# Attention scores as 128-row matmuls of zero-padded queries, with masks and biases added by VectorE

## The chip, the cores and the metric

The kernel runs on one core of one Trainium2 chip. The metric is device time in microseconds (us), the median of the runs of one build. Engines are called by the names of the profile: PE (TensorE matmul), PEld (the weight loads of TensorE, which overlap PE), DVE (VectorE), ACT (ScalarE), POOL (GpSimd), SP (SyncE, which issues most DMAs).

## The reference, cut to what matters

Two transformer blocks over 256 tokens of width 1024, float32. Block 1 has two layers. A layer projects its input into five branches (sparse, latent and differential attention, a gated unit, attention over a memory), gates, merges and adds them. Block 2 has a gated linear attention, a block-sparse attention with relative-position biases, a modulation from a condition vector, and an MLP. The attentions have 8 heads over 256 keys. Four of them add something to the scores ahead of the softmax:

```
differential, latent:  s = (q . k) * scale ; s = where(key <= query, s, -inf) ; p = softmax(s)
sparse:                s = (q . k) * scale ; s = where(key among the 64 chosen, s, -inf) ; p = softmax(s)
block-sparse (moba):   s = (q . k) * scale + bias[head, query, key] ; p = softmax(s)
```

Query and key have 64 dimensions in the sparse, differential and block-sparse attention, and 96 in the latent one. The sparse attention chooses its keys by an index score, made of 4 heads of 64 dimensions.

## The kernel before, in words

**The weight stream.** Every projection is cut into pieces of 512 rows by up to 512 columns of weights. A piece is loaded by SP (L359, L362), split by ACT into a rounded high part `wh` (L377) and by DVE into the rest `wl` (L378), and multiplied by PE in three products: high by high (L427), low weight by high operand (L428), high weight by low operand (L430), or L440, L442 and L443 in the other orientation. Six pieces are loaded ahead and three split ahead. Operands (the transposed rows of x) are split in the same way (ACT L575, DVE L576).

**What runs beside it.** Three lanes hold generators with everything else: preparation of queries and keys, attention, merging. After each half of a piece the program takes a step in a lane, so a few instructions of attention stand between two half pieces in the order of every engine. Engines work through their order in sequence; a scheduler can move instructions by their due times when the program is built.

**Attention.** `attention()` (L620) takes units. A unit is a tile t of 128 queries and two heads (t = 1, 256 keys) or four (t = 0, only the first 128 keys count), so that its scores fill one bank of PSUM, 512 floats a row. `soft()` calls `score` for each head, takes the row maximum over the bank (L640) and its negative times the scale (L642), and lets ACT write the exponentials with their sums (L647). One step later the exponentials are transposed on PE (L668) and copied out (ACT L671, DVE L672); one step further they multiply the values (L688). A differential unit calls `soft` twice. The memory's attention goes through the same code, with a scale that is a tile and no mask.

**Scores.** Queries and keys lie transposed, two heads of 64 dimensions on the 128 partitions. A head of 64 dimensions takes its half of the partitions: `qT[hb, ...]` against `kT[hb, ...]`, a matmul over 64 rows of the array (L938 differential, L926 sparse t = 0, L1391 moba, L894 the index). The heads of one unit lie on the same half, since they are two apart. For t = 1 the sparse attention's queries and keys are stacked as high and low parts on all 128 rows (L609, L610). The mask is added on PE by a bf16 matmul of an identity with a mask tile into the same bank: `identb` by `cmb` (L939, differential and latent), `identb` by `mb[t]` (L927, sparse). Moba's bias is added by DVE into a new tile (L637).

**The start.** POOL builds constants and then issues the DMAs of the small vectors (`first_loads`: positions, frequencies and eight vectors of gains and biases, L184 to L189), the last of which are transposed into `gT` (L211). Operand 1 of the first piece is transposed from the first half of x, operand 2 from the second half, whose DMA comes later.

Of the kernel before, what the change touches and what calls it, by code (L numbers as in the profile page):

```python
# [9 lines left out]
F32 = mybir.dt.float32  # L10
# [27 lines left out]
class Lane:  # L38
    """Work that runs beside the weight stream, a step at a time."""
# [18 lines left out]
def block_kernel(ctx: ExitStack, tc: tile.TileContext, a, out):  # L58
# [30 lines left out]
    def work(shape, tag="wk", dt=F32, bufs=None):  # L89
        n = 1  # L90
        for s in shape[1:]:
            n *= s
        own = tag in ("gains0", "gains1", "mb0", "mb1")
# [29 lines left out]
    class Operand:  # L123
        """[128 rows of K, up to 4 tiles, 256 tokens] as the sum of two float32r parts."""
# [9 lines left out]
    def urgent(f):  # L134
        """f with what it issues before what else is ready."""
# [21 lines left out]
    # ---- constants  # L157
    ident = cst.tile([128, 128], F32, name="ident")
    identb = cst.tile([128, 128], BF, name="identb")
    cmb = cst.tile([128, 128], BF, name="cmb")  # L160
# [38 lines left out]
    V.tensor_copy(identb, ident)  # L199
# [3 lines left out]
    V.tensor_scalar(cmb, cmf[:, 128:], -BIG * 0.5, MASK, op0=OP.is_lt, op1=OP.mult)  # L203
# [14 lines left out]
    def rsqrt(v, n):  # L218
        """1/sqrt of a [128, n] tile by Newton steps from a guess of the exponent's halving."""
# [17 lines left out]
    # ---- angles  # L237
# [42 lines left out]
    def rope(v, tab, half):  # L280
        """v [128, 2, heads, >= 2 half], in place on its first 2 half columns."""
# [14 lines left out]
    # ---- the weight stream  # L296
# [33 lines left out]
    def spread(first, fns):  # L330
        """Pieces that fns add, placed evenly among those from first on."""
# [91 lines left out]
    def mm_tok(ps, xo, k0, hi, lo, nk, n, first, last, t):  # L423
        """ps[128 tokens, n] += the tokens' rows of xo (K tiles k0..) times the weights."""
# [8 lines left out]
    def mm_tr(ps2, xo, hi, lo, nk, first, last, evac):  # L433
        """ps2: two banks of [128 columns, 2 column tiles, 256 tokens]."""
# [14 lines left out]
    def chunk(ap, ops, c0, n, evac, r0=0, pre=None, post=None):  # L449
        """Columns c0..c0+n of ap times the operands (4 K tiles each); evac(t, psum)."""  # L450
# [18 lines left out]
    def chunk_by_tile(ap, ops, c0, n, evac, pre=None, post=None, mid=None):  # L469
        """As chunk, with both K halves of the first 128 tokens before those of the others."""  # L470
# [27 lines left out]
    def chunk_pair(ap, ops, cols, evacs, pres=None, post=None, rows=(0, 512), by_tile=False):  # L498
        """Two chunks whose K halves alternate; by_tile: at the end the first 128 tokens come first."""
# [44 lines left out]
    # ---- transposes into operands  # L544
# [6 lines left out]
    def to_operand(src, t, xo, n=4, g=None, scale=None, k0=0):  # L551
        """src [128 tokens, n * 128] -> K tiles k0.. of xo, times a gain per row or a number."""
# [12 lines left out]
    def to_operand_g(srcs, xo, n, g, step=None):  # L565
        """srcs: two row tiles [128 tokens, n * 128] -> the K tiles of xo, times a gain per row."""
# [14 lines left out]
    def to_operand_mod(src, t, xo, am, bm, k0):  # L581
        """Transposes of src times am[:, k] plus bm[:, k]."""
# [24 lines left out]
    def stacked_mm(ps, q, hi, lo, stop=True):  # L607
        """ps = q^T (hi + lo), for q with a high and a low part and hi, lo repeated on both halves of the rows."""
        T.matmul(ps, q, hi, start=True, stop=False)  # L609
        T.matmul(ps, q, lo, start=False, stop=stop)  # L610
# [8 lines left out]
    # ---- softmax attention, one bank of scores at a time  # L619
    def attention(units, finish, nheads, dv, d=1):  # L620
        """units: (t, heads, nk, score, scale, combine, av, bias); one step works on three units."""
# [7 lines left out]
        def soft(u, heads):  # L629
            """Exponentials of one bank of scores, and the reciprocals of their sums."""  # L630
# [4 lines left out]
            if u.get("bias") is not None:  # L635
                sb = work([128, nh, nk])
                V.tensor_tensor(sb, ps, u["bias"], OP.add)  # L637
                ps = sb
            mx, rs, sm = small(nh), small(nh), small(nh)
            V.reduce_max(mx, ps, AX.X)  # L640
            if isinstance(u["scale"], float):
                V.tensor_scalar(mx, mx, -u["scale"], None, op0=OP.mult)  # L642
            else:
                V.tensor_scalar(mx, mx, u["scale"], -1.0, op0=OP.mult, op1=OP.mult)
            p = work([128, nh, nk])
            for k in range(nh):
                A.activation(p[:, k, :], ps[:, k, :], AF.Exp, bias=mx[:, k:k + 1], scale=u["scale"],  # L647
                             accum_out=sm[:, k:k + 1])
# [63 lines left out]
    # ---- state of a layer  # L712
# [5 lines left out]
    # block 1: the memory's keys and values  # L718
# [43 lines left out]
    # block 1: one layer  # L762
    def layer(l, h):
# [4 lines left out]
        def entry():  # L768
            """The scale of the layer's input rows."""
# [11 lines left out]
        # --- gated unit  # L781
# [46 lines left out]
        # --- memory  # L828
# [935 lines left out]
```

## Time and profile before

| | |
|---|---|
| median of 3 runs | 1260.48 us (1260.02 to 1261.89) |
| span of the profiled execution, first to last instruction | 1258.0 us |
| mean granted TensorE clock, share of full speed | 0.989 |
| PE busy | 1238.1 us, 98% |
| DVE busy | 908.2 us, 72% |
| ACT busy | 653.9 us, 52% |
| POOL busy | 11.4 us, 1% |
| moved by DMA | 231.31 MB, 184 GB/s in the mean |

The profiled execution's own time is what its span shows; the runs lie 2.0 to 3.9 us above the span, so a change of the span is taken for the same change of the time. Busy time of PE counts a matmul's whole latency, and neighbours overlap: two matmuls of one kind in a row take less than their two durations. What an instruction costs the stream is read from the distance between starts, not from its duration.

### The profile page before, as it was taken

Reading aid. Unit: us, or ns where it says so; the run is one execution under the profiler, and the core shown is the slowest. Engines: PE = TensorE matmul, PEld = TensorE weight load, DVE = VectorE, ACT = ScalarE, POOL = GpSimd, SP = SyncE. Lnnn points to the kernel's source line nnn. Section 1 sums busy time; section 2 is a strip of 40 time slices with the busy share of each in tenths; the row PEclk is TensorE's granted clock in tenths of the full one; section 3 lists DMA queues with packets and bytes.
Section 4 is the critical chain, followed back from the end, with each engine's and each line's share of the span. In section 5 each row is a group of like instructions: output and inputs, shape, how many; then the busy total and the mean of one; then the engine's idle time right before and its main releaser. Section 6 shows DMA issues by size and latency. Waiting matters only on the chain.

```text
span 1258.0 us, 17257 instructions
## 1 busy us (share of the span) xinstructions
PE 1238.1 (98%) x6593; PEld 1051.2 (84%) x6593; DVE 908.2 (72%) x1755; ACT 653.9 (52%) x1149; POOL 11.4 (1%) x29
## 2 busy tenths in 40 slices
PE   7999999999999999999999999999999999999997
PEld 6899888887888888898888878888878777899995
DVE  6876779757886777776886677876685867847665
ACT  5744644546565455545444655654555555545442
POOL 2000000000000000000000000000000000000000
PEclk8999999999999999999999999999998999999999
DMA  8965465454475465754566434755447725666750
GB/s 270 318 208 172 135 222 193 144 168 134 140 234 178 135 224 180 247 168 167 189 209 191 141 122 151 234 168 166 155 152 254 271 76 167 200 188 226 242 183 34
DMA packets 121283, 231.31 MB, mean 184 GB/s; under 512 B 5420, under 2 KB 17008, under 8 KB 121072
## 3 DMA queue, kind: packets, MB, share of 16 engines
q1 hardware_dynamic: 120880, 230.12, 55.6%
q8 instruction: 52, 0.85, 0.3%
q0 software_dynamic: 320, 0.08, 0.1%
q14 instruction: 31, 0.25, 0.1%
HBM read 229.10 MB, written 2.63 MB: 184 GB/s over the span
## 4 chain that ended last, share of the span: by engine, by line
PE 95%; DVE 2%; ACT 1%; DMA 1%; issue 0%; SPq 0%; ACTq 0%
PE pm L427 23%; PE pm L428 23%; PE pm L430 23%; PE pm L440 3%; PE pm L442 3%; PE pm L443 3%; PE po L688 3%; PE pm L548 3%; PE pm L938 2%; PE pm L668 2%; DMA t<-in_x_dram 1%; PE pm L939 1%; PE pm L836 1%; PE pm L1391 1%; PE pm L926 1%; PE po L430 1%
## 5 line engine op out<-in xcount | busy, mean ns | idle before, releaser
L378 DVE TENSOR_TENSOR wl<-wt,wh 128x1024 fp32r<-128x1024 f32 (+3 forms) x386 | 443.1, 1175 | 170.7 <-ACT wh L377 170.2
L427 PE MATMUL pm<-wh,hi 128*128 128x512 f32 (+4 forms) x1320 | 520.0, 395 | 4.5 <-ACT hi L594 2.5
L377 ACT ACTIVATE wh<-wt 128x1024 fp32r<-128x1024 f32 (+3 forms) x386 | 379.3, 1020 | 277.7 <-PE pm L430 172.2
L428 PE MATMUL pm<-wl,hi 128*128 128x512 f32 (+4 forms) x1320 | 509.6, 387 | 0.0
L430 PE MATMUL pm<-wh,lo 128*128 128x512 f32 (+4 forms) x1320 | 348.3, 384 | 0.0
L427 PEld LDWEIGHTS pm<-wh,hi 128*128 128x128 f32 x1320 | 251.3, 190 | 53.9 <-ACT hi L594 4.7
L428 PEld LDWEIGHTS pm<-wl,hi 128*128 128x128 f32 x1320 | 251.4, 191 | 44.4 <-DVE lo L576 0.2
L430 PEld LDWEIGHTS pm<-wh,lo 128*128 128x128 f32 x1320 | 246.5, 189 | 47.7
L440 PE MATMUL pm<-hi,wh 128*128 128x256 f32 x352 | 100.2, 285 | 0.0
L442 PE MATMUL pm<-lo,wh 128*128 128x256 f32 x352 | 99.4, 283 | 0.0
L443 PE MATMUL pm<-hi,wl 128*128 128x256 f32 x352 | 99.4, 283 | 0.0
L440 PEld LDWEIGHTS pm<-hi,wh 128*128 128x128 f32 x352 | 67.5, 192 | 0.5 <-ACT hi L575 0.2
L442 PEld LDWEIGHTS pm<-lo,wh 128*128 128x128 f32 x352 | 67.4, 192 | 0.5 <-DVE lo L576 0.2
L443 PEld LDWEIGHTS pm<-hi,wl 128*128 128x128 f32 x352 | 67.4, 192 | 0.0
L647 ACT ACTIVATE w<-pm,s 128x256 f32<-128x256 f32 (+1 forms) x96 | 39.2, 417 | 53.7 <-DVE s L642 52.1
L1320 DVE SCALAR_TENSOR_TENSOR w<-wt,cact,w 128x512 f32<-128x512 f32 x84 | 62.7, 746 | 1.9 <-DMA wt<-in_w_ada_dram 0.7
L688 PEld LDWEIGHTS po<-t,w 128*128 128x128 f32 x352 | 45.9, 191 | 3.5 <-ACT t L1563 0.7
L1134 ACT ACTIVATE t<-pm,s 128x512 f32<-128x512 f32 x40 | 27.6, 689 | 41.0 <-PE pm L430 40.3
L688 PE MATMUL po<-t,w 128*128 128x64 f32 (+1 forms) x352 | 45.1, 270 | 0.5 <-ACT t L1563 0.5
L548 PE MATMUL pm<-ident,t 128*128 128x128 f32 (+1 forms) x332 | 44.0, 273 | 1.6 <-DVE t L1270 1.6
L548 PEld LDWEIGHTS pm<-ident,t 128*128 128x128 f32 (+1 forms) x332 | 38.5, 137 | 7.7 <-issue 2.7
L617 ACT ACTIVATE j<-t 128x512 f32<-128x512 f32 (+3 forms) x60 | 28.9, 481 | 27.9 <-DVE t L1671 14.1
(285 smaller groups left out, 1052.5 us busy)
## 6 DMA issues: line engine op xcount, KB each, us to landing
wt<-in_w_in_dram SPq DMA_DIRECT2D x99, 1024.0 KB, 5.0
wt<-in_w_ff_dram SPq DMA_DIRECT2D x32, 1024.0 KB, 5.8
wt<-in_w_ada_dram SPq DMA_DIRECT2D x24, 1024.0 KB, 5.2
wt<-in_w_branch_dram SPq DMA_DIRECT2D x20, 1024.0 KB, 5.3
wt<-in_w_out_dram SPq DMA_DIRECT2D x12, 1024.0 KB, 5.1
wt<-in_mem_w_kv_dram SPq DMA_DIRECT2D x8, 1024.0 KB, 7.7
wt<-in_w_in_dram SPq DMA_DIRECT2D x4, 904.0 KB, 5.6
wt<-in_w_in_dram SPq DMA_DIRECT2D x4, 768.0 KB, 5.7
```

What stands on the lines that cost most here:

```text
L377: pin(A.activation(hv[:, ks], wv[:, ks], AF.Copy), on)
L378: pin(V.tensor_tensor(lv[:, ks], wv[:, ks], hv[:, ks].bitcast(F32), OP.subtract), on)
L427: T.matmul(ps[:, :n], xh, hi[:, i, :n], start=first and i == 0, stop=False)
L428: T.matmul(ps[:, :n], xh, lo[:, i, :n], start=False, stop=False)
L430: T.matmul(ps[:, :n], xo.lo[:, k0 + i, tsl(t)], hi[:, i, :n], start=False, stop=last and i == nk - 1)
L440: T.matmul(ps, wh, xh, start=first and i == 0 and c % 2 == 0, stop=False, skip_group_check=True)
L442: T.matmul(ps, wh, xl, start=False, stop=False, skip_group_check=True)
L443: T.matmul(ps, wl, xh, start=False, stop=last and i == nk - 1, skip_group_check=True)
L548: T.transpose(ps[:, i, :], src[:, i * w:(i + 1) * w], ident)
L647: A.activation(p[:, k, :], ps[:, k, :], AF.Exp, bias=mx[:, k:k + 1], scale=u["scale"], accum_out=sm[:, k:k + 1])
L688: T.matmul(opsum[t][:, h, :], pt[:, k * nb + b, :], u["v"](h, b), start=b == 0, stop=b == nb - 1)
L1320: V.scalar_tensor_tensor(acc, w[:, i, :], B["c"][:, k:k + 1], acc, op0=OP.mult, op1=OP.add)
```

## The change

Queries of 64 dimensions are written into tiles whose other 64 rows are zero (`qz` for the differential attention and moba, `dz` for the sparse attention's first tile and its index), and multiply the keys of both heads on all 128 rows. The zeros are written once by POOL; `padded()` writes only the rows that hold queries, one ACT instruction for each half. The mask matmuls and their two bf16 tiles are gone. The causal mask and the choice of keys (also used as tiles before, `cmf` and `mb`) and moba's bias are added by DVE's `tensor_tensor_reduce`, one instruction a head, which writes -scale times the sum to SBUF and its row minimum to `mx`; ACT's exponential then reads SBUF. The memory's attention keeps the old path. The scratch space of POOL's DMAs is set to 2048 bytes a partition (16384 by default).

```diff
+    qz = cst.tile([128, 8, 256], F32, name="qz")
+    dz = cst.tile([128, 12, 128], F32, name="dz")
+    for b, z in ((0, slice(64, 128)), (1, slice(0, 64))):
+        G.memset(qz[z, 4 * b:4 * b + 4, :], 0.0)
+        G.memset(dz[z, 4 * b:4 * b + 4, :], 0.0)
+        G.memset(dz[z, 8 + 2 * b:8 + 2 * b + 2, :], 0.0)
...
+    def padded(dst, ps, scale=1.0):
+        n = ps.shape[1]
+        for b in range(2):
+            own = slice(64 * b, 64 * b + 64)
+            A.activation(dst[own, n * b:n * b + n, :], ps[own], AF.Copy, scale=scale)
...
-            if u.get("bias") is not None:
-                sb = work([128, nh, nk])
-                V.tensor_tensor(sb, ps, u["bias"], OP.add)
-                ps = sb
             mx, rs, sm = small(nh), small(nh), small(nh)
-            V.reduce_max(mx, ps, AX.X)
-            if isinstance(u["scale"], float):
-                V.tensor_scalar(mx, mx, -u["scale"], None, op0=OP.mult)
+            p = work([128, nh, nk])
+            bias = u.get("bias")
+            if bias is not None:
+                for k in range(nh):
+                    V.tensor_tensor_reduce(out=p[:, k, :], in0=ps[:, k, :], in1=bias(k), scale=-u["scale"],
+                                           scalar=3.0e38, op0=OP.add, op1=OP.min, accum_out=mx[:, k:k + 1])
+                for k in range(nh):
+                    A.activation(p[:, k, :], p[:, k, :], AF.Exp, bias=mx[:, k:k + 1], scale=-1.0,
+                                 accum_out=sm[:, k:k + 1])
             else:
...
-                    A.activation(q0[:, 0:4, :], ps, AF.Copy)
+                    padded(dz[:, 0:8, :], ps)
...
-                    T.matmul(ps, q0[hb, hh // 2, :], q0[hb, 4, :], start=True, stop=False)
-                T.matmul(ps, identb, mb[t], start=False, stop=True)
+                    T.matmul(ps, dz[:, i, :], q0[:, 0, :], start=True, stop=True)
...
-        def causal(ps, q, k, t):
-            T.matmul(ps, q, k, start=True, stop=False)
-            T.matmul(ps[:, t * 128:(t + 1) * 128], identb, cmb, start=False, stop=True)
+        def causal(t):
+            return lambda k: cmf[:, 128 * (1 - t):]
...
-                ps = transpose4(cq[:, t, :])
-                A.activation(qT[:, :, tsl(t)], ps, AF.Copy)
+                padded(qz[:, :, tsl(t)], transpose4(cq[:, t, :]))
...
-                causal(ps, qT[hb, hh // 2, tsl(t)], kT[hb, hh // 2, 0:nk], t)
+                T.matmul(ps, qz[:, 4 * (hh % 2) + hh // 2, tsl(t)], kT[:, hh // 2, 0:nk], start=True, stop=True)
...
-    nc = bacc.Bacc("TRN2", target_bir_lowering=False, num_devices=1)
+    nc = bacc.Bacc("TRN2", target_bir_lowering=False, num_devices=1, dynamic_dma_scratch_size=2048)
```

Moba and the index are changed in the same way. In the changed kernel a line's number is 4 to 15 higher than before.

How the order changes, at three places. On PE, at the first differential unit of layer 1, the half piece ahead and then two heads of each of the unit's two banks; `t_2476` and `t_2477` are queries and keys. Before:

```order
L430 MATMUL pm_2631<-wh_2490,lo_130 128x288 x4
L938 MATMUL pm_2689<-t_2477,t_2476 128x256
L939 LDWEIGHTS identb
L939 MATMUL pm_2689<-cmb,identb 128x128
...
L938 MATMUL pm_2703<-t_2477,t_2476 128x256
```

And now:

```order
L434 MATMUL pm_2627<-wh_2487,lo_134 128x288 x4
L988 MATMUL pm_2685<-t_2473,qz 128x256 x2
L988 MATMUL pm_2697<-t_2473,qz 128x256 x2
L431 MATMUL pm_2628<-wh_2487,hi_133 128x288
```

The four heads' matmuls stand one behind the other, with no mask and no weight load of its own between them; the half pieces around them are the same.

On DVE, at the same unit, with the splits of weights (`wl`) around it. Before:

```order
L378 TENSOR_TENSOR wl_2768<-wt_2576,wh_2767 128x1024 x2
L640 TENSOR_REDUCE s_2694<-pm_2689 128x2
L642 TENSOR_SCALAR s_2694<-s_2694 128x2
L649 RECIPROCAL s_2695<-s_2696 128x2
L640 TENSOR_REDUCE s_2708<-pm_2703 128x2
L642 TENSOR_SCALAR s_2708<-s_2708 128x2
L378 TENSOR_TENSOR wl_2776<-wt_2629,wh_2775 128x1024
```

And now:

```order
L382 TENSOR_TENSOR wl_2760<-wt_2572,wh_2759 128x1024 x2
L653 ISA w_2691,s_2688<-pm_2685,cmf 128x256
L653 ISA s_2688 128x1
...
L664 RECIPROCAL s_2689<-s_2690 128x2
L653 ISA w_2703,s_2700<-pm_2697,cmf 128x256
L653 ISA s_2700 128x1
...
L382 TENSOR_TENSOR wl_2768<-wt_2625,wh_2767 128x1024
```

Each reduce with its small scaling became two pairs of instructions (four where a bank holds four heads); the second of a pair reads the accumulator into `mx`. The neighbours stayed.

On ACT, at the start, where `hi_127` and `hi_129` (before) are the operands of the first and second half of x and `wh_158` is the first piece. Before:

```order
L377 ACTIVATE wh_158<-wt_131 128x512 [waits DMAHW5_49]
L575 ACTIVATE hi_129<-pm_242,gT 128x256 [waits PE_49]
L575 ACTIVATE hi_127<-pm_173,gT 128x256 [waits DVE_49]
L377 ACTIVATE wh_158<-wt_131 128x512 [waits DMAHW6_49]
L377 ACTIVATE wh_186<-wt_138 128x1024 [waits DMAHW1_49]
```

And now, with `hi_131` and `hi_133` for the two operands and `wh_162` for the first piece:

```order
L381 ACTIVATE wh_162<-wt_135 128x512 [waits DMAHW5_49]
L579 ACTIVATE hi_131<-pm_177,gT 128x256 [waits DVE_49]
L381 ACTIVATE wh_162<-wt_135 128x512 [waits DMAHW6_49]
L381 ACTIVATE wh_190<-wt_142 128x1024 [waits DMAHW1_49]
...
L381 ACTIVATE wh_196<-wt_154 128x1024
L579 ACTIVATE hi_133<-pm_246,gT 128x256 [waits PE_49]
```

The second operand's first part, which waits for transposes of the second half of x, moved from ahead of the first piece's last part to behind the splits of the next two pieces. On PE those transposes moved in the same way behind 14 matmuls of the first piece, and on POOL the six fills stand ahead of the ten DMAs of `first_loads`.

## Rows read from the trace of the kernel before

**Rows 1.** The page, busy time of each engine.

```profile
PE 1238.1 (98%) x6593; PEld 1051.2 (84%) x6593; DVE 908.2 (72%) x1755; ACT 653.9 (52%) x1149; POOL 11.4 (1%) x29
```

**Rows 2.** Timeline of PE, a differential unit, 256 keys: start, duration, instructions.

```profile
285.15 0.70 PE L938 MATMUL pm<-t,t 64*128 64x256 f32 x2
285.78 0.23 PE L939 MATMUL pm<-cmb,identb 128*128 128x128 bf16 x1
285.94 0.70 PE L938 MATMUL pm<-t,t 64*128 64x256 f32 x2
...
288.40 0.30 PE L428 MATMUL pm<-wl,hi 128*128 128x288 f32 x1
```

**Rows 3.** Timeline of PEld at the same unit.

```profile
285.77 0.10 PEld L939 LDWEIGHTS <-identb 128*128 128x128 bf16 x1 [0.33 <-issue]
```

**Rows 4.** Timeline of PE, memory attention: 128 rows, 256 keys.

```profile
123.16 1.02 PE L836 MATMUL pm<-t,t 128*128 128x256 f32 x4
...
124.25 0.40 PE L428 MATMUL pm<-wl,hi 128*128 128x512 f32 x1
```

**Rows 5.** Timeline of PE, gated unit: 128 rows, 128 columns.

```profile
89.57 1.06 PE L817 MATMUL pm<-t,t 128*128 128x128 f32 x8
...
90.58 0.28 PE L442 MATMUL pm<-lo,wh 128*128 128x256 f32 x1
```

**Rows 6.** Timeline of PE, a sparse unit of four heads, 128 keys.

```profile
259.33 0.48 PE L926 MATMUL pm<-t 64*128 64x128 f32 x2
...
261.83 0.39 PE L428 MATMUL pm<-wl,hi 128*128 128x512 f32 x1
```

**Rows 7.** Timeline of PE, a latent unit of two heads, 256 keys.

```profile
383.47 0.59 PE L938 MATMUL pm<-t,t 96*128 96x256 f32 x2
...
384.79 0.40 PE L428 MATMUL pm<-wl,hi 128*128 128x512 f32 x1
```

**Rows 8.** Timeline of PE, a moba unit of two heads, 256 keys.

```profile
1002.49 1.13 PE L1391 MATMUL pm<-t,t 64*128 64x256 f32 x4
...
1003.88 0.40 PE L428 MATMUL pm<-wl,hi 128*128 128x512 f32 x1
```

**Rows 9.** Timeline of PE, index scores: two heads each of the two halves.

```profile
158.01 0.72 PE L894 MATMUL pm<-t 64*128 64x128 f32 x8
...
159.00 0.39 PE L428 MATMUL pm<-wl,hi 128*128 128x512 f32 x1
```

**Rows 10.** Groups of DVE and ACT by line and form: busy, mean ns, idle before.

```profile
L640 DVE TENSOR_REDUCE s<-pm 128x2 f32<-128x512 f32 x32 | 21.8, 682 | 3.6 <-PE pm L939 2.3 <-PE pm L927 1.3
L642 DVE TENSOR_SCALAR s<-s 128x2 f32<-128x2 f32 x28 | 4.7, 168 | 0.8
L637 DVE TENSOR_TENSOR w<-pm,t 128x512 f32<-128x512 f32 x6 | 4.1, 690 | 2.9 <-PE pm L1391 1.8 <-PE pm L1497 1.0
L576 DVE SCALAR_TENSOR_TENSOR lo<-pm,gT,hi 128x256 fp32r<-128x256 f32 x26 | 11.8, 477 | 5.7 <-ACT hi L575 5.7
L559 DVE SCALAR_TENSOR_TENSOR lo<-pm,gT,hi 128x128 fp32r<-128x128 f32 x16 | 4.5, 336 | 0.1
L647 ACT ACTIVATION_READ_ACCUMULATOR w<-pm,s 128x1 f32 x96 | 19.2, 200 | 0.0
```

**Rows 11.** Seven stretches with scores: busy of engines, clock, DMA share, GB/s.

```profile
283.00:312.00 29.00, 29.00 (x147) 21.45 (x146) 20.80 (x52) 16.68 (x44) 0.00 (x0) 1.00 0.45 146
...
sum 281.00, PE 280.48 PEld 230.44 DVE 186.04 ACT 153.04 POOL 2.10; mean PE 40.07 PEld 32.92 DVE 26.58 ACT 21.86 POOL 0.30
```

**Rows 12.** Timeline of the start, in brackets the idle time before and its cause.

```profile
12.29 0.45 PE L572 MATMUL pm<-ident,t 128*128 128x128 f32 x1 [2.81 <-DMA t<-in_x_dram]
...
15.82 0.84 ACT L575 ACTIVATE hi<-pm,gT 128x256 fp32r<-128x256 f32 x2 [4.49 <-PE pm L572]
```

**Rows 13.** POOL and DVE at the start: a fill, and the copy of the vectors.

```profile
0.94 0.32 POOL L200 MEMSET cmf<- 128x256 f32 x1
...
33.59 0.26 DVE L211 COPY gT<-pm 128x106 f32<-128x106 f32 x1
```

More of the change, by code (lines that the diff above doesn't have):

```diff
@@ L92, in work @@
             n *= s
-        own = tag in ("gains0", "gains1", "mb0", "mb1")
+        own = tag in ("gains0", "gains1", "mb0", "mb1", "q0")
         t = wrk.tile([128, n if own else 512], dt, tag=tag if own else "wk", name=nm("w"),
@@ L634, in soft @@
                 u["score"](ps[:, k, :], h, u["t"], nk)
-            if u.get("bias") is not None:
-                sb = work([128, nh, nk])
-                V.tensor_tensor(sb, ps, u["bias"], OP.add)
-                ps = sb
             mx, rs, sm = small(nh), small(nh), small(nh)
-            V.reduce_max(mx, ps, AX.X)
-            if isinstance(u["scale"], float):
-                V.tensor_scalar(mx, mx, -u["scale"], None, op0=OP.mult)
+            p = work([128, nh, nk])
[7 more added lines that the diff above has]
+                                 accum_out=sm[:, k:k + 1])
             else:
+                V.reduce_max(mx, ps, AX.X)
                 V.tensor_scalar(mx, mx, u["scale"], -1.0, op0=OP.mult, op1=OP.mult)
[L645 to L648, printed above, removed]
+                for k in range(nh):
+                    A.activation(p[:, k, :], ps[:, k, :], AF.Exp, bias=mx[:, k:k + 1], scale=u["scale"],
+                                 accum_out=sm[:, k:k + 1])
             V.reciprocal(rs, sm)
@@ L875, in dsa_prep @@
                 else:
-                    V.tensor_copy(q0[:, 4:8, :], ps)
+                    V.tensor_copy(q0, ps[:, 0:2, :])
+                    padded(dz[:, 8:12, :], ps[:, 2:4, :])
                 for _ in range(3):
@@ L889, in dsa_prep @@
                     for p in range(2):
-                        hb = slice(64 * b, 64 * b + 64)
                         if t:
@@ L893, in dsa_prep @@
                         else:
-                            T.matmul(ps[:, p, :], q0[hb, 6 + p, :], q0[hb, 5, :], start=True, stop=True)
+                            T.matmul(ps[:, p, :], dz[:, 8 + 2 * b + p, :], q0[:, 1, :], start=True, stop=True)
                     R[b] = work([128, 2, nk], "P")
@@ L999, in diff_attn @@
             units = [dict(t=t, heads=[2 * i for i in os_], heads2=[2 * i + 1 for i in os_], outs=os_,
-                          nk=128 * (t + 1), score=score, scale=64 ** -0.5,
+                          nk=128 * (t + 1), score=score, scale=64 ** -0.5, bias=causal(t),
                           combine=combine, v=lambda hh, b: cv[:, b, hh * 128:(hh + 1) * 128])
@@ L1088, in score @@
             def score(ps, hh, t, nk):
-                causal(ps, L["mqT"][hh // 4][:, hh % 4, tsl(t)], L["mkT"][hh // 4][:, hh % 4, 0:nk], t)
-            units = [dict(t=t, heads=hs, outs=hs, nk=128 * (t + 1), score=score, scale=96 ** -0.5,
+                T.matmul(ps, L["mqT"][hh // 4][:, hh % 4, tsl(t)], L["mkT"][hh // 4][:, hh % 4, 0:nk], start=True,
+                         stop=True)
+            units = [dict(t=t, heads=hs, outs=hs, nk=128 * (t + 1), score=score, scale=96 ** -0.5, bias=causal(t),
                           v=lambda hh, b: L["mv"][:, b, hh * 64:(hh + 1) * 64])
@@ L1382, in moba_prep @@
             yield
-        B["mT"] = (qT, kT)
+        B["mT"] = kT
     def moba_attn():
-        qT, kT = B["mT"]
+        kT = B["mT"]
         o = slot([128, 2, 512])
         def score(ps, hh, t, nk):
-            hb = slice(64 * (hh % 2), 64 * (hh % 2) + 64)
-            T.matmul(ps, qT[hb, hh // 2, tsl(t)], kT[hb, hh // 2, 0:nk], start=True, stop=True)
+            T.matmul(ps, qz[:, 4 * (hh % 2) + hh // 2, tsl(t)], kT[:, hh // 2, 0:nk], start=True, stop=True)
         units = []
@@ L1395, in moba_attn @@
                 hs = (4 * q + p, 4 * q + p + 2)
-                units.append(dict(t=1, heads=hs, bias=B["bias"][p][:, 2 * q:2 * q + 2, :]))
+                units.append(dict(t=1, heads=hs, bias=lambda k, p=p, q=q: B["bias"][p][:, 2 * q + k, :]))
         for p in range(2):
-            units.append(dict(t=0, heads=(p, p + 2, p + 4, p + 6), bias=B["bias"][p][:, :, 128:256]))
+            units.append(dict(t=0, heads=(p, p + 2, p + 4, p + 6),
+                              bias=lambda k, p=p: B["bias"][p][:, k, 128:256]))
         for u in units:
```

28 lines of the change are left out of this document (11 added, 17 removed).

## The prediction

> **What bounds the kernel now.** I read the page's busy times first, then PE's timeline at each place where scores are made, and only then DVE's groups. PE is busy 98% of the span, DVE 72%, ACT 52% [rows 1]; over the seven stretches that hold the masked scores PE has 280.48 of 281 us, and DVE 186.04 [rows 11]. So a microsecond that PE does not need is a microsecond of the span, as long as DVE and ACT keep up, and a microsecond added to DVE costs nothing until DVE is full. Busy PE is not PE at its peak, however: what counts is how far the starts lie apart.
>
> In a differential unit a head takes 0.79 us from one first matmul to the next (285.15, 285.94) [rows 2]. The mask matmul in between is a small one of 128 bf16 columns, and it does not explain this: the weight load ahead of it sits idle 0.33 us with no releaser but issue, after 64-row matmuls [rows 3]. With 128 rows, no mask and the same 256 keys, the memory's attention needs 1.09 us from its first matmul to the second matmul behind it for two heads [rows 4]; that span includes one matmul of the stream, about 0.23 us, so a head takes 0.43. The weight of the next matmul is there in time. What costs is the passage from 64-row to 128-row use and back, twice a head, and not the columns.
>
> **PE, the scores.** All counts are 2 layers by 8 heads for each tile. I compare like spans, from the first score to the second matmul of the stream behind.
> - Differential, t = 1: 0.79 now, 0.43 after, by the rows above. 16 heads by 0.36: 5.8 us.
> - Differential and sparse, t = 0 (128 keys). Four sparse heads take 259.33 to 261.83, 2.50 us [rows 6]. Eight instructions of 128 rows and 128 columns, as many as four padded heads have, take 89.57 to 90.58, 1.01 us [rows 5]; the stream's matmul in that span has 256 columns and not 512, so I add 0.11 and compare with 1.12. That saves 1.38 a unit, 0.345 a head; 32 heads: 11.0 us.
> - Latent, both tiles, and sparse, t = 1: already 96 or 128 rows, so only the mask goes. Two latent heads take 383.47 to 384.79, 1.32 us [rows 7], against 1.09: 0.115 a head. 48 heads, the sparse ones and t = 0 taken alike: 5.5 us.
> - Moba has no mask matmul. Its four instructions take 1002.49 to 1003.88, 1.39 us [rows 8], against 1.09: 0.30 for entering and leaving, six units, 1.8 us.
> - The index, twice, mixes the halves: eight instructions in 0.99 us [rows 9] against 1.12, so padding loses 0.13 each, 0.3 us.
>
> Sum: 5.8 + 11.0 + 5.5 + 1.8 - 0.3 = 23.8 us. Bounds: at least the masks alone, 96 by 0.115 = 11 us, if padded queries bring back none of the switching; at most about 28 if moba's later units and the t = 0 heads switch oftener than the rows shown.
>
> The index rows speak of a rule against the change. The Trainium skill ("TensorE: Matmul & The Clock Gate", Part 3: Packing small matmuls) holds that short-K matmuls on different row groups run concurrently, so that padding them to 128 rows throws away up to half. The trace agrees in the one place where halves alternate, and there the gain was 0.13 us and not half; by the rule in full the index would lose 0.45 us each time, and the sum would be 23.2. Elsewhere a unit's heads share one half, and there is nothing to give up.
>
> **DVE, the extremes.** There are 36 masked banks (12 differential and 12 latent, 12 sparse over both layers). Each loses a reduce of 0.682 and a small scaling of 0.168 us, 30.6 us in all; moba's six lose the bias addition as well, 6 by (0.690 + 0.682 + 0.168) = 9.2 [rows 10]. Together 39.8. What comes is one instruction a head with an accumulator read behind it: 112 pairs, 56 of 256 columns and 56 of 128. The trace has no such instruction. The nearest rows are three-operand ones that read PSUM: 0.477 for 256 columns and 0.336 for 128; the read lies between the smallest DVE instruction, 0.168, and ACT's own accumulator read, 0.200 [rows 10]. Below, instructions in a row overlap a little and a pair might take 0.36, which would make the exchange free; above, I have no row, so the rival below asks how dear a pair must be. I take 0.65 and 0.51: 56 by 1.16 = 65 us, 25 more than now.
>
> A page has a lower price in a sentence of its own. The Trainium skill ("VectorE: DVE Perf Modes", The TRN2 errata) gives a fixed part per instruction plus its columns, 392 and 258 ns here as an estimate, by which the instructions alone would come to 36 us; it also warns that many small instructions pay the fixed part each, which is this change's direction, and no row of this trace can show it for this instruction.
>
> This load lies beside PE. The seven stretches would be 281 - 24 = 257 us long and hold 186 - 40 + 65 = 211 us of DVE work, 82% against 66% now. The tightest is the differential stretch: 20.8 of 29.0 us [rows 11], less six banks' 5.1, plus 8 by 0.65 and 8 by 0.51, makes 25.0 us in about 23.2. So there DVE falls behind by some 2 us, and what is late next is the split of weights queued behind the pairs, for which PE would wait; three pieces split ahead are the cover, each 24 matmuls of 0.23 us, and they take it unless the stretch behind is full too. I charge 1 us for both layers, at most 4.
>
> ACT writes queries in two instructions instead of one, and its exponentials read SBUF. That is some 8 us over the whole kernel on an engine that is idle 48% [rows 1]. The bank of scores is now freed by DVE and not by ACT, which is earlier. I take nothing for either; without the cover it would be the 8 us.
>
> **The start.** ACT stood 4.49 us (until 15.82) ahead of the second operand's first part, because PE's transposes waited 2.81 us for x [rows 12]. Behind that ACT instruction were the last part of piece 0 and the splits of pieces 1 and 2, for which PE was waiting in turn, and piece 3's load waited for the buffer of piece 0. In the new order these stand ahead of it, and PE has 14 matmuls of piece 0 ahead of its own wait for x. What can come back lies between nothing (if piece 0's last part lands no earlier) and 4.49; I take 2.8, PE's own wait.
>
> Against it, POOL fills 2 by 1792 columns ahead of the small vectors' DMAs. A fill of 256 columns took 0.32 [rows 13], so at most 14 by 0.32 = 4.5 us. The vectors were used first at 33.59 [rows 13], long after they were asked for in the first microseconds; I take nothing, and 4.5 us if they had no slack at all. The smaller scratch space bears on ten small DMAs only, within the same bound.
>
> **The sum.** -23.8 (scores) - 2.8 (start) + 1 (waits for splits) = -25.6. The span of 1258.0 becomes 1232.4. The shown runs' median lies 2.5 us above the profiled span, so the same subtraction from 1260.48 gives 1234.9; I say 1235. About 0.2%, 2.5 us, is what a measurement of this kernel can tell from no change.
>
> **The rivals.**
> - *DVE fills up locally.* The differential stretch is over its length by my price, and the stream behind it is dense. If a pair costs 0.9 us, the seven stretches hold 146 + 101 = 247 of 257 us and the differential one 15.7 + 14.4 = 30 of 23; the two differential stretches then give back about 7 us each, less some 2 each for the cover. Time: about 1245. For it: no row prices the pair. Against: nothing of its width on DVE takes that long. 0.12.
> - *The other side: DVE becomes the bound.* From (257 - 146) / 112 = 0.99 us a pair on, all seven stretches are full; at (281 + 2.8 - 146) / 112 = 1.23 us the gain is used up, and at 1.35 the stretches take 297 us, 16 more than now, less 2.8: about 1274. It would take an instruction that runs at half the rate and an accumulator read of several tenths. Against: the nearest rows are at half this price. 0.04.
> - *The change does not do what it says on PE.* If the idle weight loads come from the bf16 load itself or the 64-row matmuls cost as much when padded, only the masks' 11 us come back: 1260.5 - 11 - 2.8 = about 1247. For it: the idle load in [rows 3] belongs to the mask. Against: moba has no mask and still loses 0.30 a unit [rows 8], and latent heads have the mask and lose only 0.115 [rows 7]. 0.06.
> - *The start gives nothing or takes.* Vectors late by the fills, no earlier split: 1235 + 2.8, up to 1242. 0.10.
>
> The forecast itself, 1230 to 1240, has 0.66; 0.02 is left for less than 1230 (more switching in the scattered units than shown). All cases but the second rival and a part of the first and third lie below 1258, so faster 0.92, same 0.04, slower 0.04. The range, 1226 to 1247, takes in the first and third rival's times.
>
> **What would show it.** PE: padded heads of 256 keys 0.43 us apart, of 128 keys 0.22, no idle weight load there, PE's count of matmuls down by the 96 masks. DVE: pairs at 0.65 and 0.51, busy near 930 us; PE's waits for `wl` after the differential stretches about 1 us in all. Start: ACT's wait of 4.49 gone. The forecast is wrong if PE waits for DVE in the score stretches, if a pair is near 1 us, or if the padded heads keep a distance of 0.6 or more.

## The result, and the profile after

The changed kernel takes 1232.58 us (median of 4 runs, 1231.84 to 1232.80) against 1261.18 for the kernel before on the same chip: a ratio of 0.9778, interval 0.9764 to 0.9792. The forecast was 1235. The profiled span went from 1258.0 to 1230.5 us, 27.5 less, and 1.9 below that run's time of 1232.42.

The page's busy times after, to be read beside [rows 1]:

```profile
PE 1211.6 (98%) x6497; PEld 1044.2 (85%) x6497; DVE 903.7 (73%) x1887; ACT 664.5 (54%) x1161; POOL 14.8 (1%) x35
```

PE is still what is busy all the time, with 96 matmuls fewer. DVE has 132 instructions more and is busy 4.5 us *less*; 25 more was forecast.

PE's timeline after, at the sparse unit of [rows 6], the differential one of [rows 2], the latent one of [rows 7] and the moba one of [rows 8]:

```profile
257.94 1.06 PE L941 MATMUL pm<-w,dz 128*128 128x128 f32 x8
...
259.06 0.39 PE L432 MATMUL pm<-wl,hi 128*128 128x512 f32 x1
...
280.82 1.89 PE L988 MATMUL pm<-t,qz 128*128 128x256 f32 x8
...
282.69 0.30 PE L432 MATMUL pm<-wl,hi 128*128 128x288 f32 x1
...
373.37 1.03 PE L1100 MATMUL pm<-t,t 96*128 96x256 f32 x4
...
374.48 0.40 PE L432 MATMUL pm<-wl,hi 128*128 128x512 f32 x1
...
977.21 1.03 PE L1401 MATMUL pm<-t,qz 128*128 128x256 f32 x4
...
978.31 0.39 PE L432 MATMUL pm<-wl,hi 128*128 128x512 f32 x1
```

From the first score to the second matmul of the stream: differential 1.87 us for four heads (3.25 before, 285.15 to 288.40), sparse 1.12 (2.50), latent 1.11 (1.32), moba 1.10 (1.39). These are the spans that the prediction set against each other: sparse, latent and moba come within 0.02 us of what it put there (1.12, 1.09, 1.09), and the differential one is 0.06 longer (four heads by 0.36 less would be 1.81).

DVE's groups after, in the place of those of [rows 10]:

```profile
L653 DVE CUSTOM_DVE_ANT_0 w<-pm,cmf 128x256 f32<-128x256 f32 x32 | 12.3, 417 | 0.8 <-PE pm L1100 0.6
L653 DVE DVE_READ_ACCUMULATOR2_ANT s<- 128x1 f32 x112 | 9.3, 83 | 0.0
L653 DVE CUSTOM_DVE_ANT_0 w<-pm,cmf 128x128 f32<-128x128 f32 x32 | 7.3, 284 | 0.1
```

The fused instruction takes 0.417 us for 256 columns and 0.284 for 128, with 0.083 for the read, a pair of 0.50 or 0.37 us.

To see where the 27.5 us come from I compared, in each trace, the starts of the same first product (L427, or its line in the other kernel) of the stream, of which every kernel here has the same 1352. Differences between neighbouring marks are lengths of stretches; the marks lie around the attentions. In us, worked out from the traces; the columns behind the first two are experiments below.

```
stretch                  before  changed  pad_only  mask_only  diff_64
start, to about 64 us     63.82    63.56     63.47      62.85    64.96
to about 200             135.89   135.87    135.86     135.90   135.91
sparse, layer 1           71.20    67.24     69.15      68.04    67.24
differential, layer 1     36.09    30.23     32.02      29.38    29.34
latent, layer 1          135.06   133.19    135.07     134.03   134.03
between the layers       246.32   245.96    246.39     245.89   245.96
sparse, layer 2           28.86    25.38     26.82      26.16    25.38
differential, layer 2     43.16    37.33     39.09      36.47    36.43
latent, layer 2           99.82    97.98     99.82      98.00    98.01
start of block 2          59.06    59.06     59.06      59.06    59.06
next, to before moba      67.15    66.74     66.69      62.64    65.59
moba                      49.41    45.68     47.14      47.38    45.66
rest                     222.19   222.22    222.23     222.22   222.22
```

The seven stretches of the attentions give 26.6 us: sparse 7.4, differential 11.7, latent 3.7, moba 3.7. The start gives 0.3, "between the layers" and "next, to before moba" 0.4 each, and none loses more than 0.03. So the time came back where it was forecast, except at the start.

The start itself, the timeline of ACT, beside [rows 12]:

```profile
10.09 0.62 ACT L381 ACTIVATE wh<-wt 128x512 fp32r<-128x512 f32 x1
13.68 2.01 ACT L381 ACTIVATE wh<-wt 128x1024 fp32r<-128x1024 f32 x2 [2.97 <-DMA wt<-in_w_in_dram]
```

and that of PE some 40 us later:

```profile
54.33 1.36 PE L576 MATMUL pm<-ident,t 128*128 128x128 f32 x11
55.45 0.36 PE L444 MATMUL pm<-hi,wh 128*128 128x256 f32 x1
58.74 0.39 PE L446 MATMUL pm<-lo,wh 128*128 128x256 f32 x1 [2.93 <-DVE lo L580]
```

The last part of piece 0 is split at 10.09, and no longer behind the wait of 4.49 us for PE that [rows 12] show. Piece 0's last products start at 14.62, where they started at 20.57 before. Of this lead nearly 5 us are there when piece 1 ends; near 55 us PE waits 2.93 us for a low part that DVE has not written. DVE's queue at that place:

```profile
54.76 1.22 DVE L382 TENSOR_TENSOR wl<-wt,wh 128x1024 fp32r<-128x1024 f32 x1
...
56.09 1.00 DVE L815 TENSOR_SCALAR t<-t,s,s 128x512 f32<-128x512 f32 x2
57.00 1.29 DVE L817 TENSOR_TENSOR t<-t,w 128x512 f32<-128x512 f32 x2
58.21 0.48 DVE L580 SCALAR_TENSOR_TENSOR lo<-pm,gT,hi 128x256 fp32r<-128x256 f32 x1
```

The low part stands behind a split of the memory's weights and four instructions of the gated unit. DVE had come to this stage only 1.4 us earlier than before (58.21 against 59.62).

POOL's fills and the copy of the vectors, beside [rows 13]:

```profile
1.99 0.95 POOL L205 MEMSET qz<- 64x1024 f32 x1
...
30.29 0.26 DVE L215 COPY gT<-pm 128x106 f32<-128x106 f32 x1
```

The six fills stand from 1.99 to 5.37, 3.4 us, and the copy came at 30.29 and not later: the slack was there.

### The profile page after: what moved, and what is told of

Same layout as the page of the kernel before. It is cut to its first block, busy times and chain, and to the rows that moved or that the text cites. A ratio compares the mean times of both kernels' runs of the same rounds, so it can differ in the third digit from the quotient of the medians.

```text
span 1230.5 us, 17201 instructions
## 1 busy us (share of the span) xinstructions
PE 1211.6 (98%) x6497; PEld 1044.2 (85%) x6497; DVE 903.7 (73%) x1887; ACT 664.5 (54%) x1161; POOL 14.8 (1%) x35
## 4 chain that ended last, share of the span: by engine, by line
PE 91%; DVE 4%; ACT 1%; DMA 1%; issue 1%; SPq 0%; ACTq 0%
PE pm L431 22%; PE pm L432 22%; PE pm L434 22%; PE pm L446 3%; PE pm L444 3%; PE pm L447 3%; PE po L703 3%; PE pm L552 3%; DVE wl L382 2%; PE pm L683 2%; DMA wt<-in_w_in_dram 1%; PE pm L1100 1%; PE pm L988 1%; PE pm L851 1%; PE po L434 1%
## 5 line engine op out<-in xcount | busy, mean ns | idle before, releaser
L656 ACT ACTIVATE w<-w,s 128x256 f32<-128x256 f32 (+1 forms) x112 | 49.9, 446 | 39.0 <-DVE s L653 39.0
L1146 ACT ACTIVATE t<-pm,s 128x512 f32<-128x512 f32 x40 | 27.5, 688 | 43.6 <-PE pm L434 43.6
```

The lines of the kernel that those rows point to most:

```text
L656: A.activation(p[:, k, :], p[:, k, :], AF.Exp, bias=mx[:, k:k + 1], scale=-1.0, accum_out=sm[:, k:k + 1])
```

## The experiments

Two theories were set against each other first. P, the prediction's: a passage between 64-row and 128-row use costs, and padding takes it away. M: the cost belongs to the mask, whatever the rows.

**pad_only.** Padding alone, masks back on PE.

```diff
-                    T.matmul(ps, dz[:, i, :], q0[:, 0, :], start=True, stop=True)
+                    T.matmul(ps, dz[:, i, :], q0[:, 0, :], start=True, stop=False)
+                T.matmul(ps, identb, mb[t], start=False, stop=True)
```

and the same for `causal`, with the old reduce and moba's bias addition.

> Queries padded as in the change, but masks still added on PE by the bf16 identity matmul, row extremes and moba's bias by the old DVE instructions. Theory P (what costs is the passage between 64-row and 128-row use; a mask by itself costs 0.115 us): a masked differential head of 256 keys goes from 0.79 to 0.545 us, one of 128 keys loses 0.23, moba gives its whole part: 3.9 + 7.4 + about 3 - 0.3 = 14 us, 1246 to 1249. Theory M (the cost belongs to the mask's own weight load, whatever the rows): masked heads stay at 0.79 and 0.57, only moba gains, 1257 to 1260.

1243.07 us, ratio 0.9862 (0.9839 to 0.9885), which is below P's range of 1246 to 1249; single runs go from 1238.77 at a mean clock of 0.996 to 1245.04 at 0.991. The attentions give 14.5 us where P said 14: sparse 4.1, differential 8.1, latent nothing, moba 2.3. PE's timeline at the first differential unit:

```profile
282.64 0.59 PE L952 MATMUL pm<-t,qz 128*128 128x256 f32 x2
283.07 0.22 PE L953 MATMUL pm<-cmb,identb 128*128 128x128 bf16 x1
283.12 0.65 PE L952 MATMUL pm<-t,qz 128*128 128x256 f32 x2
283.61 0.22 PE L953 MATMUL pm<-cmb,identb 128*128 128x128 bf16 x1
283.67 0.65 PE L952 MATMUL pm<-t,qz 128*128 128x256 f32 x2
```

A head with its mask takes 0.55 us, as the latent one did, and not 0.79. The mask is the same and only the rows differ, so M is out: the 0.24 us belong to the passage.

**mask_only.** Masks, biases and extremes on DVE, queries on 64 rows.

```diff
-            T.matmul(ps, q, k, start=True, stop=False)
-            T.matmul(ps[:, t * 128:(t + 1) * 128], identb, cmb, start=False, stop=True)
+            T.matmul(ps, q, k, start=True, stop=True)
```

and `soft` as changed.

> Masks, biases and extremes on DVE as in the change, queries still on 64 rows. Theory P: between the heads of a group there is no passage any more, but each of ten groups and six moba units pays 0.30 for entering and leaving: 5.5 (masks of 96 and 128 rows) + 16.8 (the 64-row heads) - 3.0 = 19 us, 1240 to 1244; a differential unit of four heads takes about 2.0 us instead of 1.72. Theory M: everything but moba's part, 1238 to 1240, four heads in 1.72.

1230.20 us, ratio 0.9773 (0.9757 to 0.9790): as fast as the whole change, within both intervals, 10 us faster than P allowed and 8 faster than M, of which the clock has some 4 (below). The attentions give 24.1 us with not a query padded. PE's timeline at the first differential unit, and at a sparse unit of four heads:

```profile
281.06 1.14 PE L940 MATMUL pm<-t,t 64*128 64x256 f32 x8
282.13 0.40 PE L427 MATMUL pm<-wh,hi 128*128 128x288 f32 x1
282.37 0.29 PE L428 MATMUL pm<-wl,hi 128*128 128x288 f32 x1
...
257.36 1.16 PE L929 MATMUL pm<-t 64*128 64x128 f32 x8
258.44 0.50 PE L427 MATMUL pm<-wh,hi 128*128 128x512 f32 x1
258.79 0.40 PE L428 MATMUL pm<-wl,hi 128*128 128x512 f32 x1
```

and PEld's, behind the differential unit:

```profile
282.13 0.19 PEld L427 LDWEIGHTS pm<-wh,hi 128*128 128x128 f32 x1 [0.33 <-issue]
```

Four differential heads take 1.31 us, not the 2.0 that P expected and not M's 1.72; padded they take 1.87. Their eight instructions start in pairs, 0.013 us apart (281.064 and 281.078, then 281.384 and 281.398, 281.599 and 281.613), from the second pair on a pair every 0.215 us: two heads run at once. The unit's two banks hold heads of opposite halves (`heads` even, `heads2` odd), which mask and passage had kept apart before. A sparse unit's heads share one half: its eight start one by one, 0.11 us apart, and take 1.43 where the padded ones take 1.12. The rule of the Trainium skill that the prediction set aside ("TensorE: Matmul & The Clock Gate", Part 3: Packing small matmuls), that short-K matmuls on different row groups run concurrently, agrees with these rows. A passage in and out costs some 0.31 us a group (1.43 less 1.12), as moba's unit showed. The idle 0.33 us of [rows 3] stand here ahead of a load of the stream's own weights, with no bf16 weight load in the unit: they belong to the passage, against the prediction's third rival. Whether sparse and moba units would gain from heads of both halves was not tried.

So the two halves of the change do not add: 14.5 alone, 24.1 alone, 26.6 together. In the stretch before moba this run is 4.1 us shorter than the change, and that is the clock's (below).

**ttr_twice and ttr_thrice.** How much DVE could take.

```diff
-                for k in range(nh):
+                for k in [k for k in range(nh) for _ in range(2)]:
                     V.tensor_tensor_reduce(out=p[:, k, :], in0=ps[:, k, :], in1=bias(k), scale=-u["scale"],
```

(3 for the second kernel.)

> The changed kernel with each of the 112 pairs of DVE instructions (add, scale and minimum; accumulator read) issued twice with the same result, 112 more pairs at 0.50 or 0.37 us: 48 us more of DVE. Theory P (PE sets the time, DVE lies beside it): at most 3 us more, 1232 to 1236. Rival (DVE is nearly full where scores are made): the differential stretch then holds some 30 us of DVE work in 23, and both layers give back 4 to 6 us each, 1240 to 1245.

1242.46 us, ratio 0.9860 (0.9846 to 0.9875): 9.9 more than the change, so the expectation of at most 3 was wrong. But nor did the differential stretches fill: they are 30.23 and 37.30 us, as in the change. In the profiled execution 9.4 of it lie in the latent stretch of layer 1 (142.58 against 133.19) and 1.1 in moba's, and the 9.4 are one place, behind the last differential unit. PE's timeline there:

```profile
311.10 1.07 PE L434 MATMUL pm<-wh,lo 128*128 128x512 f32 x4
316.44 0.71 PE L703 MATMUL po<-t,w 128*128 128x128 f32 x4 [4.28 <-ACT w L686]
319.77 0.58 PE L703 MATMUL po<-t,w 128*128 128x128 f32 x1 [2.62 <-DVE w L687]
```

and two stretches around it, with the granted clock behind the five busy times:

```profile
306.00:316.00 10.00, 6.16 (x32) 4.89 (x30) 7.59 (x25) 7.62 (x18) 0.00 (x0) 1.00 0.52 163
316.00:326.00 10.00, 6.94 (x28) 6.08 (x29) 9.40 (x29) 3.35 (x13) 0.00 (x0) 0.66 0.16 53
```

The unit's chain of extreme, exponential, transpose and copy became longer than the half pieces put between its steps. PE then waits 4.28 and 2.62 us, and in the second stretch the granted clock is 0.66 in the mean, for a part of it the lower of its two levels, 1.2 GHz. The last accumulator read of that unit on DVE, in this run and then in the change:

```profile
312.09 0.08 DVE L653 DVE_READ_ACCUMULATOR2_ANT s<- 128x1 f32 x1
...
302.11 0.08 DVE L653 DVE_READ_ACCUMULATOR2_ANT s<- 128x1 f32 x1
```

It comes 10 us later. The unit's eight more pairs are some 2 us of that (a pair every 0.21 us); the builder also ordered the instructions anew, and four splits of weights of 1.22 us each now stand among the unit's pairs, where the change has none. Nor is it the load of a stretch: between the marks DVE is busy 0.90 of the second differential stretch and 0.89 of the second latent one, which lose nothing and 0.3 us, and 0.81 of the one that loses 9.4. What the length of the chain and what its new order did was not parted.

> The same, each pair issued three times: 97 us more of DVE, a pair in effect 1.3 us. By the prediction's threshold of 0.99 us a pair all score stretches are then full: 146 + 146 = 292 us of DVE work in 254, so 25 to 40 us more than the changed kernel if nothing moves out of the stretches, 1258 to 1272; if the splits ahead carry half of it, 1245 to 1255. If DVE has no part in the time at all it stays under 1236.

1280.86 us, ratio 1.0168 (1.0153 to 1.0183), slower than the kernel before and 9 above the highest that was expected. The latent stretches lose 17.6 and 13.3 us against before, moba 10.1. A pair at 1.3 us is past the point where the gain is used up, as the second rival said, but the stretches are not full: DVE is busy between 0.72 and 0.88 of each of the seven. PE's waits are again for the units' own chains (7.3 us for DVE L997, 6.7 for ACT L686, 6.5 for the exponentials) and hardly for splits of weights (0.4), and the mean clock is 0.978, against 0.990 in the change.

**two_ops.** The fused instruction taken apart.

```diff
-                    V.tensor_tensor_reduce(out=p[:, k, :], in0=ps[:, k, :], in1=bias(k), scale=-u["scale"],
-                                           scalar=3.0e38, op0=OP.add, op1=OP.min, accum_out=mx[:, k:k + 1])
+                    V.tensor_tensor(p[:, k, :], ps[:, k, :], bias(k), OP.add)
+                V.reduce_max(mx, p, AX.X)
+                V.tensor_scalar(mx, mx, -u["scale"], None, op0=OP.mult)
```

> The changed kernel with the fused instruction taken apart: an addition per head, one maximum over the bank, one small scaling. A bank of two heads then takes 2 x 0.42 + 0.68 + 0.17 = 1.69 us of DVE instead of 1.0, one of four 1.99 instead of 1.48: 27 us more of DVE. If the reserve of DVE is what the doubled pairs showed (48 us more cost 9.7, all in one latent stretch), this costs between 0 and 6 us, 1232 to 1239; if the time follows DVE's load in proportion, 5.4; if DVE had ample reserve, nothing.

1241.62 us, ratio 0.9849 (0.9834 to 0.9863): 9 more than the change, where 0 to 6 were expected. In the profiled execution 9.4 of it lie in the moba stretch (55.11 against 45.68). PE's timeline:

```profile
992.30 1.12 PE L704 MATMUL po<-t,w 128*128 128x64 f32 x8 [0.47 <-ACT w L687]
996.90 0.86 PE L684 MATMUL pm<-ident,w 128*128 128x128 f32 x2 [3.48 <-ACT w L657]
```

and the stretch behind it:

```profile
995.00:1005.00 10.00, 8.10 (x24) 4.71 (x25) 5.74 (x25) 2.03 (x9) 0.53 (x1) 0.50 0.34 106
```

One wait of 3.48 us for exponentials, then ten us at the lower clock level (0.50). DVE's load is not it: DVE is busy 0.71 of the moba stretch, less than in the change (0.75). The scores and transposes of the last unit, in the change and then in this run:

```profile
987.05 1.06 PE L1401 MATMUL pm<-t,qz 128*128 128x128 f32 x8
991.54 0.61 PE L683 MATMUL pm<-ident,w 128*128 128x128 f32 x4
...
991.33 0.39 PE L1402 MATMUL pm<-t,qz 128*128 128x128 f32 x2
```

In the change a half piece of the stream stands between scores and transposes; here the builder put it ahead of the scores, and only the values' matmuls at 992.30 stand between. So this run shows what a chain with nothing beside it costs, and not the price of three instructions in the place of one: their longer chain and the new order were not parted.

**fills_late.** The start in the old order, by fills behind the small DMAs.

```diff
+        first_loads()
+        for b, z in ((0, slice(64, 128)), (1, slice(0, 64))):
+            G.memset(qz[z, 4 * b:4 * b + 4, :], 0.0)
...
```

> The changed kernel with POOL's six fills behind the DMAs of the small vectors, which puts the start back in the old order (second operand's first part ahead of the last part of piece 0). Theory S (the new order's head start of some 5 us is given back before 64 us, so it is worth nothing): the first operand product at 60 us stands where it stands in the changed kernel within 0.7 us, no wait of 2.9 us for a low part, 1232 to 1233.5. Rival (the head start is worth what was predicted): 2.8 us more, 1235 to 1236.

1231.72 us (1227.75 to 1232.70), ratio 0.9774 (0.9761 to 0.9788). The mark at 64 us comes at 63.21, before 63.82, changed 63.56, and the wait for the low part is gone. It was the fills that made the new order, since that edit alone brings the old one back. The new order was worth nothing against this execution of the change, and 1.4 us against a second one (`changed_again`, 61.78). Those two differ by the clock: over the first 64 us the mean granted clock is 0.95 in the change and in fills_late, 0.92 before, and 1.00 in changed_again.

**tables.** Sine and cosine behind the tanh on ACT.

```diff
+        while "silu" not in marks:
+            yield
+        with behind("silu"):
+            A.activation(sin.rearrange("p a b -> p (a b)"), r, AF.Sin)
```

> The changed kernel with the sine and cosine of the angles put behind the condition vector's tanh on ACT, so that one table load of 1.28 us goes from the stretch around 37 us, ahead of a split of weights whose raw buffer the memory's first weights wait for. If that split is what gives back the head start, PE's wait of 2.9 us near 56 us shrinks by about 1.3 and the time is 1231 to 1232; if the wait comes from DVE's own queue or from the DMAs, it stays and the time is 1232.6.

1230.47 us, ratio 0.9763 (0.9749 to 0.9776). PE's wait near 56 us became two of 1.2 us each, and the mark at 200 us comes at 197.34, 2.1 earlier than in the change. But `changed_again` has 197.65 there with the wait as it was (2.72 us), at the same clock: 1.00 over the first 64 us in both, 0.95 in the change's first execution. So at one clock the edit is worth 0.3 us of the 2.1; the rest goes with the clock. At the mark at 64 us the edit is 1.7 ahead of changed_again (60.04 and 61.78), of which the next stretch takes 1.4 back (137.30 and 135.87).

**diff_64.** Padding taken back where two halves can run at once.

```diff
-                padded(qz[:, :, tsl(t)], transpose4(cq[:, t, :]))
+                A.activation(qT[:, :, tsl(t)], ps, AF.Copy)
...
-                T.matmul(ps, qz[:, 4 * (hh % 2) + hh // 2, tsl(t)], kT[:, hh // 2, 0:nk], start=True, stop=True)
+                T.matmul(ps, qT[hb, hh // 2, tsl(t)], kT[hb, hh // 2, 0:nk], start=True, stop=True)
```

> The changed kernel with the differential attention's queries back on 64 rows, unpadded; sparse, index and moba stay padded. Theory C (without masks the two halves of a differential unit run at the same time, which padding gave up; the other padded scores gain from having no passage): each differential stretch 0.85 us shorter than in the changed kernel, the other stretches the same, 1230.5 to 1231.5, unless the clock's dip after 900 us falls otherwise, which is worth up to 4 us either way. Theory P (padding gains everywhere): each differential stretch longer by at least 0.30 for every group, 1234 or more.

1231.15 us, ratio 0.9765 (0.9752 to 0.9779). The differential stretches are 29.34 and 36.43 us, 0.89 and 0.90 shorter than in the change, as theory C (heads of the two halves run at the same time) said. The latent stretch of layer 1 gives 0.84 back, in a wait of PE for DVE of 0.7 us, so 0.95 us remain, less than the medians can tell.

**best and changed_again.** Both edits together, beside the change once more.

> The changed kernel with both edits that gained: differential queries on 64 rows, and the angles' sine and cosine behind the tanh. By the stretches of the single edits: two differential stretches 0.9 us shorter each, a wait of 0.7 us in the latent stretch behind the first, and about 2 us kept from the start: 3 us less than the changed kernel run beside it, apart from the clock's dip after 900 us. If the two starts don't add to the scores' part, 1 us less.

> The changed kernel as it is, on the same chip as the run before it, for the size of the spread between executions: the same median within 1 us of 1232.6, single runs between 1228 and 1233 as the clock falls or not after 900 us.

1226.84 us (1225.05 to 1230.01), ratio 0.9742 (0.9729 to 0.9756), against 1231.49 (1230.41 to 1232.92), ratio 0.9775 (0.9762 to 0.9789). This is the fastest version of the study; its slowest run lies below the fastest of the change beside it. By stretches, though, only 0.9 us of that are the scores; 4.2 are the stretch before moba, 62.35 against 66.55, and the start, of which some 2 us were to be kept, takes 1.5 back up to 200 us (a mean clock of 0.95 over the first 64 us, against 1.00). The stretch before moba differs by the clock. Two pieces of it in the changed kernel:

```profile
903.00:908.00 5.00, 5.00 (x20) 4.00 (x19) 4.02 (x25) 0.92 (x2) 0.00 (x0) 0.74 0.46 176
918.00:928.00 10.00, 10.00 (x45) 9.23 (x46) 3.33 (x6) 3.41 (x7) 0.00 (x0) 0.56 1.00 304
```

and in mask_only, whose PE does the same work there:

```profile
903.00:908.00 5.00, 4.83 (x26) 3.83 (x26) 4.93 (x28) 2.09 (x6) 0.00 (x0) 1.00 0.47 179
918.00:928.00 10.00, 10.00 (x52) 8.47 (x52) 2.08 (x3) 3.03 (x6) 0.59 (x1) 0.83 0.95 308
```

PE waits 1.40 and 1.11 us between 898 and 903 in both. Behind these waits the granted clock fell in the one execution and stayed up in the other; between 918 and 928 it fell in both, further in the first. From 898 to 935 its mean is 0.82 in the change and in changed_again, and 0.95 in mask_only, fills_late and best. The same program shows both: five executions of fills_late have mean clocks from 0.994 down to 0.989 and times from 1227.75 up to 1232.70. Why `best` kept its clock up in all five (0.993 to 0.997) was not settled.

## Why the prediction was right, step by step

**The sum.** It came out by errors of opposite sign: the scores gave 2.8 us more than forecast and the start 2.5 less, and the 1 us for waits was not needed.

**The scores.** Forecast 23.8 us, measured 26.6. Sparse 7.4 (its terms 5.5 + 1.8), differential 11.7 (5.8 + 5.5) and latent 3.7 (3.7) are as summed. Moba was mis-sized: 1.8 forecast, 3.7 measured, since its scores of 128 keys stood between transposes, entering and leaving several times, and the one row the term was made from did not. In mask_only, with queries on 64 rows, moba gives 2.0 of the 3.7: there the builder put these transposes together ahead of the scores. The index, as forecast, takes 1.12 us and not 0.99.

**What the gain belongs to.** Here a step failed, though the sum did not: "Elsewhere a unit's heads share one half, and there is nothing to give up." A differential unit calls `soft` for even and then for odd heads, so its two banks lie on opposite halves, and mask_only and diff_64 show that they run at once when nothing stands between. Padding therefore costs 0.9 us in each differential stretch. The index could have told: in the trace of the kernel before its matmuls start in pairs too, the first two at 158.010 and 158.024.

```profile
158.01 0.39 PE L894 MATMUL pm<-t 64*128 64x128 f32 x2
```

Its 0.99 us are to be set against the 1.43 that eight such matmuls of one half take in mask_only. That is 0.44 us from running two at a time; the prediction set them against the padded 1.12, where the passage hides most of it, and read 0.13. That passages cost was right (pad_only), that padding was what recovers them was half right: the masks' move alone took away most passages. That the named cause gave the right size is therefore luck in part: 24.1 us come without any padding. Padding's own part beside it is 26.6 - 24.1 = 2.5 us, and with the latent wait of mask_only taken out (0.84) some 1.6.

**DVE.** A pair was priced at 0.65 and 0.51; it is 0.50 and 0.37 with its read of 0.083, and overlap (in a row a pair starts every 0.35 or 0.21 us) makes DVE's busy time 4.5 us smaller rather than 25 larger. The accumulator read was the term furthest off. The charge of 1 us for waits was not needed.

**DVE's reserve.** The first rival, that DVE fills locally, had its price right (pairs doubled to about 0.9 us: 1242.46 measured, about 1245 forecast) and its mechanism wrong: the stretches that DVE fills most lose nothing, PE waits for the chain of one unit in the order that the builder gave it, and the clock then adds to the wait. The second rival's threshold of 1.23 us a pair fits ttr_thrice, slower at 1.3 in effect, but its reason does not: DVE is never busy more than 0.88 of a stretch there.

**The start.** Forecast 2.8, measured 0.3 and, in the second execution, 2.0; between the two lies the clock. The wait on ACT went as told, and a lead of 5 us was there; what was left out is that a lead is kept only if every engine behind it can run earlier too, and DVE came to the low part only 1.4 us earlier.

**ACT, POOL.** Nothing was charged, and no loss shows: ACT is 10.6 us busier at 54%, the fills take 3.4 us, the copy of the vectors comes earlier than before, and no score waits.

## What to carry to other kernels

Look at what stands between two short-K matmuls before changing their shape. A small matmul of another shape in the middle can cost more than its columns, by the weight load that is not done ahead, and once it is gone the short ones may run two at a time, so that padding them is a loss where neighbours lie on opposite halves with separate banks, and a gain of about 0.3 us a group where they share one half. Judge an engine off the critical path by the longest chain it is part of, and by what stands among the steps of that chain, and not by its mean load, and compare stretches of the same work rather than medians when the clock moves the total by as much as the edit.

## What the runs showed of the hardware that was not expected

- The fused add, scale and minimum with its accumulator costs 0.417 us for 256 columns from PSUM, less than the three-operand instruction of [rows 10] at 0.477; its read takes 0.083, less than half of the 0.168 and 0.200 that stood in for it.
- Waits of PE cost more than their length: after waits of 4.28 and 2.62 us the clock averaged 0.66 over ten us, after one of 3.48 it was 0.50 over ten us. The latent stretch of ttr_twice lost 9.4 us against the change (142.58 and 133.19) with 6.9 us of waits, and the moba stretch of two_ops 9.4 with 4.0.
- One program's executions differ by up to 6.3 us (pad_only, 1238.77 to 1245.04) with its mean clock (0.996 and 0.991), while seven of the kernel before beside them spread by 2.0 (1258.96 to 1260.98).
